# HGRN's levels and the DeltaNet inverse's block products as matmuls of 32 columns, in four strips of the array

## The chip, the core and the metric

The kernel runs on one core of one Trainium2 chip. The metric is the device time of one execution in microseconds; the median of three runs stands for a kernel, and one more execution was profiled. TensorE (PE in the profile; its weight loads are listed apart as PEld) does matmuls into PSUM, VectorE (DVE), ScalarE (ACT) and GpSimd (POOL) work on what it leaves, SyncE (SP) issues the DMAs.

## The reference, cut to what matters

One layer of a decoder trunk: 2048 tokens of width 1024, in f32. After an input projection, four heads go through a gated delta rule (DeltaNet) and four through HGRN2; then come the output projection, an MLP and a gated embedding. The change touches the inside of the two mixers.

```python
# DeltaNet, per chunk of tokens
decay = exp(where(causal, gc[:, None] - gc[None, :], -inf))
lmat  = (k_beta @ k.T) * decay
a_mat = eye + where(strict, lmat, 0)          # unit lower triangular
u, w  = solve(a_mat, v_beta), solve(a_mat, k_beta * exp(gc))
...
# HGRN2, per chunk: a decay for every one of the 128 state channels d
pair = exp(where(causal, b[:, None] - b[None, :], -inf))
att  = einsum('id,jd,ijd->ij', q, k, pair)
o    = att @ v + (q * exp(b)) @ s
...
# what follows
mix = concat(o_a, o_b);  h = x + rms_norm(mix @ w_out)
h  = h + rms_norm(square(relu(rms_norm(h) @ w_up)) @ w_down)
out = h + e * sigmoid(h @ w_gate)
```

## The kernel before

All large products run as matmuls of 128 rows by 128 weight columns by 512 moving columns, with operands split into a high and a low f32r part (`mm`, `mmo`, `u`, `d`, `mmg` in the profile). The small products inside the mixers are plain f32 (`F32` tiles); one of these in the program is two matmuls, each with a weight load, in the trace.

The work goes quarter by quarter (`q`, 512 tokens, four chunks of 128). For each head eight projections of 24 large matmuls are run; after every eighth of these matmuls (`tick`), and half way between (`half`), an agenda lets the generators of the mixers go one step further. So TensorE's order is written by hand: projections of one head with the short products of heads before strewn in, at the places that `A_STEPS` (DeltaNet, `gdn_mixer`) and `B_STEPS` (HGRN, `hgrn_mixer`) name. TensorE and SyncE run in that order; VectorE's, ScalarE's and GpSimd's order in the mixers is set by a scheduler.

*HGRN.* `att` of a chunk of 128 tokens is made in levels, s = 1, 2, 4, ..., 64 (`LEVELS`): at each, pairs of blocks of s tokens, late queries against early keys, both multiplied up to the border between the blocks. The first step of the loop (`lev == 1`) multiplies each chunk's 128 keys with the odd halves of the queries for s = 1 and s = 2 at once (2 x 64 columns, `both`), the others multiply 128 packed `keys` with the 2 x 64 late queries, for two c. Of these products only blocks on the diagonal are wanted; a mask (`mask[lev]`) lets just those through when VectorE copies them to `att` (`copy_predicated`). At s = 4, 8, 16 and 32 a strip of 32 keys meets only 32 of the 128 columns; at s = 64 it is all.

*DeltaNet.* The inverse of the triangular matrix of 128 is made from inverses of its 32-blocks (`xn`, and transposed `xt`), which VectorE solves. Two steps then join blocks to 64 (`um[5]`, `part[5]`: `psp5`, `psx5`, `pst5`) and to 128 (`um[6]`, `part[6]`: `psp6`, `psd6`); each product is run by `pairs` for two pairs of chunks with all 128 weight columns, and ScalarE or VectorE copies out the blocks of 32 or 64 that are wanted.

*PSUM.* Eight banks of [128, 512] f32: `pm` 2 (projections), `po` 2 (outputs), `pp` 4, from which norms, transposes, the DeltaNet products and all HGRN levels (`at_...`) take a bank in turn.

Of the kernel before, what the change touches and what calls it, by code (L numbers as in the profile page):

```python
# [10 lines left out]
F32 = mybir.dt.float32  # L11
# [6 lines left out]
PSUM = bass.MemoryType.PSUM  # L18
DRAM = bass.MemoryType.DRAM

P = 128
# [3 lines left out]
QT = 512  # L25
NQ = T // QT
NC = QT // P
# [4 lines left out]
SB = 32  # L32
NB = P // SB
# [63 lines left out]
def trunk(ctx, tc, x, xT, pT, vecs, w_in, w_ab, gdn_a_log, gdn_dt_bias, w_out, w_up, w_down,  # L97
          w_ple, w_gate, consts, out):
    nc = tc.nc
    V, S, G, PE = nc.vector, nc.scalar, nc.gpsimd, nc.tensor  # L100
# [6 lines left out]
    sm = ctx.enter_context(tc.tile_pool(name="sm", bufs=3))  # L107
    dr = ctx.enter_context(tc.tile_pool(name="dr", bufs=1, space=DRAM))
    pm = ctx.enter_context(tc.tile_pool(name="pm", bufs=2, space=PSUM))
    pp = ctx.enter_context(tc.tile_pool(name="pp", bufs=4, space=PSUM))  # L110
    ph = pp
    po = ctx.enter_context(tc.tile_pool(name="po", bufs=2, space=PSUM))

    def bank(name, pool=None):
        return (pool or pm).tile([P, QT], F32, tag="ps", name=name)

    def blk(c):
        return slice(c * P, (c + 1) * P)

    mixers = ctx.enter_context(ExitStack())  # L120
    cm = mixers.enter_context(tc.tile_pool(name="cm", bufs=1))
    cst = cm.tile([P, N_CONST, P], F32, name="cst")
    rows = cp.tile([N_ROWS, P], F32, name="rows")
# [333 lines left out]
    with mixers as mctx:  # L457
# [12 lines left out]
        um = {lev: mp.tile([P, NC // 2, P], F32, name=f"um{lev}") for lev in (5, 6)}  # L470
        part = {lev: mp.tile([P, NC // 2, P], F32, name=f"part{lev}") for lev in (5, 6)}
# [148 lines left out]
        halves = [slice(0, P // 2), slice(P // 2, P)]  # L620

        def rows_of(g):
            return slice(g * SB, (g + 1) * SB)

        def gdn_mixer(q, h, live):

            n = f"g{q}_{h}"
# [8 lines left out]
            both = sm.tile([P, 2, NC], F32, tag="tail", name=f"tail_{n}")  # L636
# [111 lines left out]
            V.transpose(flat(xt), flat(xn))  # L748
            yield

            def pairs(out, lhsT, rhs):
                for p in range(2):
                    PE.matmul(out[:, p], lhsT[:, p], rhs[:, p], start=True, stop=True)

            def two(t):
                return t.rearrange("p (n two) i -> p n (two i)", two=2)
# [3 lines left out]

            def ends(t):
                return bass.AP(t.tensor, t.offset, [list(t.ap[0]), [P, 2], [3 * SB, 2], [1, SB]])

            def half_bank(name):
                return bank(f"{name}_{n}", pp)[:, : QT // 4].rearrange("p (a i) -> p a i", a=2)

            psp = half_bank("psp5")
            pairs(psp, um[5], ends(xn))  # L770
            for g in range(NB):
                S.activation(part[5][rows_of(g), :, rows_of(g ^ 1)], psp[rows_of(g), :, rows_of(0 if g % 2 else 1)],
                             AF.Copy)
            yield
            psx, pst = half_bank("psx5"), half_bank("pst5")
            pairs(psx, two(xt), ends(part[5]))
# [20 lines left out]
            for c in range(NC):  # L797
                s = state[h]
# [38 lines left out]
        def hgrn_mixer(q, h, live):  # L837
# [26 lines left out]
            for lev, s in enumerate(LEVELS):  # L864
# [4 lines left out]
                if lev == 1:  # L869
                    ps0 = bank(f"at_{n}_d", ph)[:, : QT // 2]  # L870
                    PE.matmul(ps0, one, own, start=True, stop=True)
                    ps1 = bank(f"at_{n}_{lev}", ph).rearrange("p (c n) -> p c n", c=NC)
                    for c in range(NC):
                        PE.matmul(ps1[:, c, :], k[:, blk(c)], both[:, :, c * P // 2 : (c + 1) * P // 2],
                                  start=True, stop=True)
                    chunks = ps1.rearrange("p (a b) n -> p a b n", a=2)
                    eye = bass.AP(ident.tensor, ident.offset, [list(ident.ap[0]), [1, 2], [0, 2], [2, P // 2], [1, 1]])
                    V.tensor_tensor(side_of_chunks(columns_of, 1, False),
                                    ps0.rearrange("p (a b n s) -> p a b n s", a=2, b=2, s=1), eye, ALU.mult)
                    V.tensor_tensor(side_of_chunks(columns_of, 1, True), chunks[:, :, :, : P // 2, None],  # L880
                                    mask[0][:, None, None, :, None].broadcast_to([P, 2, 2, P // 2, 1]), ALU.mult)
                    ps = chunks[:, :, :, P // 2 :]
                else:

                    ps = bank(f"at_{n}_{lev}", ph)[:, : QT // 2].rearrange("p (a b n) -> p a b n", a=2, b=2)
                    for c in range(2):
                        queries = bass.AP(qq.tensor, qq.offset + c * P + s,
                                          [list(qq.ap[0]), [QT // 2 - s, 2], [2 * s, P // (2 * s)], [1, s]])
                        PE.matmul(ps[:, :, c, :], keys[:, blk(c)], queries, start=True, stop=True)  # L889
# [229 lines left out]
        with tc.manual_schedule(engines={mybir.EngineType.SP}):  # L1119
# [826 lines left out]
```

## Time and profile before

| | |
|---|---|
| median of 3 runs | 2665.27 us (2663.72 to 2666.59) |
| profiled execution | 2665.86 us, span of its instructions 2664.1 us |
| PE busy | 2637.0 us (99%), 12745 matmuls |
| PEld (weight loads) busy | 2209.8 us (83%) |
| DVE / ACT / POOL busy | 1968.0 us (74%) / 1468.8 us (55%) / 136.4 us (5%) |
| granted TensorE clock | 1.00 throughout |
| DMA | 573.51 MB, mean 215 GB/s |

The profile is of one execution. Busy time of PE counts overlapping matmuls once, from the start of one to its modelled end, so that 99% says that TensorE is never without work and not that it works at its peak. In rows of groups the columns are: line, engine, operation, output<-inputs, rows*columns of the array and the moving operand, count | busy us, mean ns of one | idle us of the engine before them. In rows of the timeline: start in us from the span's start, us, engine, line, operation, and so on. The mixers run from about 66 to 1107 us; the rest of the output projection, the MLP and the gate follow.

### The profile page before, as it was taken

What the parts mean: (1) busy time and instruction counts of PE and PEld (TensorE: products, weight loads), DVE (VectorE), ACT (ScalarE), POOL (GpSimd) and SP (SyncE); (2) the same over time, 40 slices, a digit from 0 to 9 for tenths busy, and PEclk for the clock granted to TensorE, in tenths of its full rate; (3) what the DMA queues carried; (4) which work ended last, traced back from release to release, by engine and by line L of the source; (5) the groups of instructions that cost most, each with busy time, mean ns of one, the idle gap of its engine ahead of it and who ended that gap; (6) DMA issues with size and microseconds to landing.
All of it is one profiled execution on the core that took longest, in us unless ns stands there. A gap on an engine that the chain in (4) does not pass through costs nothing.

```text
span 2664.1 us, 38284 instructions
## 1 busy us (share of the span) xinstructions
PE 2637.0 (99%) x12745; PEld 2209.8 (83%) x12745; DVE 1968.0 (74%) x4029; ACT 1468.8 (55%) x2991; POOL 136.4 (5%) x147
## 2 busy tenths in 40 slices
PE   8999999999999999999999999999999999999999
PEld 6888888888888888877888888888888888888887
DVE  7778777786677677578988867767877765468775
ACT  6666555465455456566565555555554555565431
POOL 0000000000000000010000000001000001101000
PEclk9999999999999999999999999999999999999999
DMA  8787777667666775682766476666544465677663
GB/s 281 274 261 256 241 268 238 227 225 240 218 212 221 234 220 176 203 250 102 242 213 202 164 242 219 213 204 207 199 171 145 160 236 187 198 253 250 209 224 124
DMA packets 267766, 573.51 MB, mean 215 GB/s; under 512 B 55578, under 2 KB 60152, under 8 KB 250416
## 3 DMA queue, kind: packets, MB, share of 16 engines
q1 hardware_dynamic: 265264, 566.86, 63.9%
q0 software_dynamic: 2304, 4.20, 0.9%
q8 instruction: 101, 1.65, 0.3%
q14 instruction: 97, 0.79, 0.1%
HBM read 410.57 MB, written 160.37 MB: 214 GB/s over the span
## 4 chain that ended last, share of the span: by engine, by line
PE 60%; DMA 3%; DVE 2%; ACT 1%; issue 1%; SPq 0%; POOL 0%; DVEq 0%; ACTq 0%; POOLq 0%
PE d L1171 23%; PE u L1171 23%; PE mmg L1171 7%; PE mm L1139 3%; PE mmo L1022 1%; PE mme L199 1%; DMA mixT<-mixd 1%; DMA yod<-yo 1%; DMA yo<-in_xT_dram 0%; DVE t L173 0%; DVE acc_o L242 0%; DMA sys_g<-ud_g 0%; DMA wd<-in_w_down_dram 0%; PE at_h L889 0%; DMA ud_g<-u_g 0%
## 5 line engine op out<-in xcount | busy, mean ns | idle before, releaser
L1139 PE MATMUL mm<-xt,w 128*128 128x512 f32 x3072 | 783.6, 400 | 1.3 <-DVE w L173 0.8
L1139 PEld LDWEIGHTS mm<-xt,w 128*128 128x128 f32 x3072 | 553.3, 189 | 102.0 <-issue 1.3
L1171 PE MATMUL d<-db,da 128*128 128x512 f32 x2688 | 612.8, 389 | 0.0
L1171 PEld LDWEIGHTS d<-db,da 128*128 128x128 f32 x2688 | 504.5, 188 | 104.8
L1171 PE MATMUL u<-t,wu 128*128 128x512 f32 x2604 | 591.2, 389 | 0.0
L1171 PEld LDWEIGHTS u<-t,wu 128*128 128x128 f32 x2604 | 488.7, 188 | 101.5
L226 DVE TENSOR_TENSOR db<-db 128x512 fp32r<-128x512 f32 x224 | 159.3, 711 | 58.5 <-ACT db L225 57.9
L1569 DVE TENSOR_TENSOR u<-u,u 128x512 f32<-128x512 f32 x224 | 150.1, 681 | 51.3 <-PE u L1171 49.7
L225 ACT ACTIVATE db<-db 128x512 fp32r<-128x512 f32 x224 | 141.0, 629 | 65.6 <-DMA db<-hid 60.4
L1171 PE MATMUL mmg<-h2T,wg 128*128 128x512 f32 (+1 forms) x792 | 174.7, 383 | 0.0
L1171 PEld LDWEIGHTS mmg<-h2T,wg 128*128 128x128 f32 x792 | 145.5, 188 | 29.1
L1612 ACT ACTIVATE u<-u 128x512 f32<-128x512 f32 x128 | 80.8, 631 | 152.3 <-DVE u L1569 151.6
L173 DVE TENSOR_TENSOR da<-da 128x512 fp32r<-128x512 f32 x128 | 95.4, 745 | 88.8 <-ACT da L172 85.5
L172 ACT ACTIVATE da<-da 128x512 fp32r<-128x512 f32 x128 | 80.5, 629 | 126.1 <-DMA da<-sumd 106.5
L1171 PE MATMUL mmo<-mixT,w_out 128*128 128x512 f32 x600 | 138.4, 390 | 1.5 <-DVE w_out L173 1.1
L1171 PEld LDWEIGHTS mmo<-mixT,w_out 128*128 128x128 f32 x600 | 112.2, 188 | 26.6 <-DVE w_out L173 2.3
L172 ACT ACTIVATE wu<-a 128x512 fp32r<-128x512 f32 x124 | 75.1, 624 | 54.6 <-DMA a<-in_w_up_dram 52.7
L173 DVE TENSOR_TENSOR wu<-a,wu 128x512 fp32r<-128x512 f32 x124 | 85.8, 694 | 9.3 <-ACT wu L172 9.1
L173 DVE TENSOR_TENSOR da<-dr,da 128x512 fp32r<-128x512 f32 x96 | 68.2, 710 | 22.9 <-ACT da L172 21.4
L1613 ACT ACTIVATE u<-u 128x512 f32<-128x512 f32 x128 | 80.4, 628 | 3.0
L172 ACT ACTIVATE da<-dr 128x512 fp32r<-128x512 f32 x96 | 60.5, 631 | 30.5 <-DMA dr<-in_w_down_dram 19.6
L242 POOL TENSOR_TENSOR acc_y<-acc_y,sq_y 128x512 f32<-128x512 f32 x28 | 37.9, 1355 | 757.8 <-ACT sq_y L241 757.8
(391 smaller groups left out, 3810.8 us busy)
## 6 DMA issues: line engine op xcount, KB each, us to landing
w<-cache_in SPq DMA_DIRECT2D x96, 1024.0 KB
db<-hid SPq DMA_DIRECT2D x224, 256.0 KB
cache_in<-w SPq DMA_DIRECT2D x32, 1024.0 KB
hid<-u SPq DMA_DIRECT2D x128, 256.0 KB
da<-sumd SPq DMA_DIRECT2D x128, 256.0 KB
a<-in_w_up_dram SPq DMA_DIRECT2D x124, 256.0 KB
hid<-ht SPq DMA_DIRECT2D x96, 256.0 KB
dr<-in_w_down_dram SPq DMA_DIRECT2D x96, 256.0 KB
```

Of the source, the lines that this page charges most:

```text
L172: S.activation(t[:, 0], raw, AF.Copy)
L173: eng.tensor_tensor(t[:, 1], raw, t[:, 0], ALU.subtract)
L199: PE.matmul(ps, a, b, start=i == 0, stop=i == n - 1)
L225: S.activation(t[:, 0], plain(t), AF.Copy)
L226: V.tensor_tensor(t[:, 1], plain(t), t[:, 0], ALU.subtract)
L242: eng.tensor_tensor(acc, acc, sq, ALU.add)
L1022: PE.matmul(ps, w[:, term // 2, k, :], xin[q][k][:, term % 2, :], start=i == 0, stop=i == 3 * KD - 1)
L1139: PE.matmul(ps, *terms[i], start=i == 0, stop=i == nt - 1)
L1171: PE.matmul(ps, a, b, start=start, stop=stop)
L1569: V.tensor_tensor(c[new], c[old], ps, ALU.add)
L1612: S.activation(c[k], c[k], AF.Relu)
L1613: S.activation(c[k], c[k], AF.Square)
```

## The change

The products of the levels up to s = 32, and all block products of the inverse, are no longer matmuls of 128 weight columns. A new helper `strip(g, ...)` runs a matmul of 32 weight columns at column position 32 g of the array, which writes PSUM's partitions 32 g to 32 g + 31; a product is given as four strips, and each strip gets only those moving columns that are read later: 32 of 128 in the levels, 32 of 64 or 64 of 128 in the inverse. Blocks that nobody reads are left out (`psx5`: two strips, not four). The level s = 64 stays as it was.

The levels no longer take a bank from `pp`: they write one bank of their own, `at_all`, set to zero once; the first step uses all of it, those after it its two halves in turn. `pp` has three banks while the mixers run, and four again (a new pool) behind them. What VectorE and ScalarE do with the results is the same.

```diff
-    pp = ctx.enter_context(tc.tile_pool(name="pp", bufs=4, space=PSUM))
-    ph = pp
...
+    pp = mixers.enter_context(tc.tile_pool(name="pp", bufs=3, space=PSUM))
+    ph = pp
+    at_all = mixers.enter_context(tc.tile_pool(name="pa", bufs=1, space=PSUM)).tile([P, QT], F32, name="at_all")
+    V.memset(at_all, 0.0)
...
+        def strip(g, out, lhsT, rhs):
+
+            PE.matmul(out, lhsT, rhs, start=True, stop=True, tile_position=(0, g * SB))
...
-            def pairs(out, lhsT, rhs):
+            def in_halves(out, lhsT, rhs, other):
                 for p in range(2):
-                    PE.matmul(out[:, p], lhsT[:, p], rhs[:, p], start=True, stop=True)
+                    for g in range(NB):
+                        to = halves[g // 2 ^ other]
+                        strip(g, out[rows_of(g), p, to], lhsT[:, p, rows_of(g)], rhs[:, p, to])
...
-            pairs(psp, um[5], ends(xn))
+            for p in range(2):
+                for g in range(NB):
+                    strip(g, psp[rows_of(g), p, rows_of(1 - g % 2)], um[5][:, p, rows_of(g)],
+                          two(xn)[:, p, rows_of(0 if g % 2 else NB - 1)])
...
-            pairs(psx, two(xt), ends(part[5]))
-            pairs(pst, part[5], two(xt)[:, :, SB : 3 * SB])
+            for p in range(2):
+                for g in range(NB):
+                    strip(g, pst[rows_of(g), p, rows_of(g % 2)], part[5][:, p, rows_of(g)],
+                          two(xt)[:, p, rows_of(1 + g % 2)])
+                for g in (1, 2):
+                    strip(g, psx[rows_of(g), p, rows_of(g - 1)], two(xt)[:, p, rows_of(g)],
+                          part[5][:, p, rows_of(0 if g == 1 else NB - 1)])
...
-            pairs(psp, um[6], two(xn))
+            in_halves(psp, um[6], two(xn), 1)
...
-            pairs(psd, part[6], two(xt))
+            in_halves(psd, part[6], two(xt), 0)
...
-                    ps1 = bank(f"at_{n}_{lev}", ph).rearrange("p (c n) -> p c n", c=NC)
+                    near = [slice(j * SB // 2, (j + 1) * SB // 2) for j in range(NB)]
+                    ps1 = at_all.rearrange("p (c n) -> p c n", c=NC)
                     for c in range(NC):
-                        PE.matmul(ps1[:, c, :], k[:, blk(c)], both[:, :, c * P // 2 : (c + 1) * P // 2],
-                                  start=True, stop=True)
+                        for j in range(NB):
+                            strip(j, ps1[rows_of(j), c].rearrange("p (l n) -> p l n", l=2)[:, :, near[j]],
+                                  k[:, c * P + j * SB : c * P + (j + 1) * SB],
+                                  both[:, :, c * P // 2 : (c + 1) * P // 2][:, :, near[j]])
...
-                    ps = bank(f"at_{n}_{lev}", ph)[:, : QT // 2].rearrange("p (a b n) -> p a b n", a=2, b=2)
+                    ps = at_all[:, lev % 2 * QT // 2 : (lev % 2 + 1) * QT // 2].rearrange("p (a b n) -> p a b n", a=2, b=2)
                     for c in range(2):
-                        queries = bass.AP(qq.tensor, qq.offset + c * P + s,
-                                          [list(qq.ap[0]), [QT // 2 - s, 2], [2 * s, P // (2 * s)], [1, s]])
-                        PE.matmul(ps[:, :, c, :], keys[:, blk(c)], queries, start=True, stop=True)
+                        start = qq.offset + c * P + s
+                        if 2 * s == P:
+                            queries = bass.AP(qq.tensor, start, [list(qq.ap[0]), [QT // 2 - s, 2], [1, s]])
+                            PE.matmul(ps[:, :, c, :], keys[:, blk(c)], queries, start=True, stop=True)
+                            continue
+                        for j in range(NB):
+                            out = ps[rows_of(j), :, c, near[j]]
...
+                            strip(j, out, keys[:, c * P + j * SB : c * P + (j + 1) * SB], queries)
...
+    pp = ctx.enter_context(tc.tile_pool(name="pq", bufs=4, space=PSUM))
```

Two places of TensorE's order show it. The first is in the first quarter, where the projections of head 1 carry the second level of head 0's HGRN (`at_h_0_2`), a transpose of head 1's keys (`t_kg`), and then the first block product of head 0's inverse (`psp`) with the third level. Rows give line, output<-inputs, output rows x moving columns, and how many in a row. Before:

```order
L1139 MATMUL mm_0_1_1289<-xt_2_489,w_0_1_1158 128x512 x2
L889 MATMUL at_h_0_2_1298<-qk_h_0_978,keys_h_0_1_1254 128x2x64 x2
L1139 MATMUL mm_0_1_1289<-xt_2_489,w_0_1_1158 128x512
L1139 MATMUL mm_0_1_1289<-xt_3_506,w_0_1_1158 128x512 x3
L1139 MATMUL mm_0_1_1289<-xt_4_522,w_0_1_1158 128x512 x3
L1139 MATMUL mm_0_1_1289<-xt_5_538,w_0_1_1158 128x512
L595 MATMUL t_kg_1_1319<-cst,y_kg_1_1216 128x128 x4
L1139 MATMUL mm_0_1_1289<-xt_5_538,w_0_1_1158 128x512 x2
L1139 MATMUL mm_0_1_1289<-xt_6_554,w_0_1_1158 128x512 x3
L1139 MATMUL mm_0_1_1289<-xt_7_557,w_0_1_1158 128x512 x3
L753 MATMUL psp_g_0_1349<-xn_g_0_1202,um_575 128x64 x2
L889 MATMUL at_h_0_3_1356<-qk_h_0_978,keys_h_0_2_1302 128x2x64 x2
```

The same place in the changed kernel, where the line of all strips is that of the helper, L629:

```order
L1167 MATMUL mm_0_1_1305<-xt_2_494,w_0_1_1163 128x512 x2
L629 MATMUL at_all<-qk_h_0_983,keys_h_0_1_1270 32x2x16 x8
L1167 MATMUL mm_0_1_1305<-xt_2_494,w_0_1_1163 128x512
L1167 MATMUL mm_0_1_1305<-xt_3_511,w_0_1_1163 128x512 x3
L1167 MATMUL mm_0_1_1305<-xt_4_527,w_0_1_1163 128x512 x3
L1167 MATMUL mm_0_1_1305<-xt_5_543,w_0_1_1163 128x512
L597 MATMUL t_kg_1_1340<-cst,y_kg_1_1221 128x128 x4
L1167 MATMUL mm_0_1_1305<-xt_5_543,w_0_1_1163 128x512 x2
L1167 MATMUL mm_0_1_1305<-xt_6_559,w_0_1_1163 128x512 x3
L1167 MATMUL mm_0_1_1305<-xt_7_562,w_0_1_1163 128x512 x3
L629 MATMUL psp_g_0_1370<-xn_g_0_1207,um_580 32x32 x8
L629 MATMUL at_all<-qk_h_0_983,keys_h_0_2_1323 32x2x16 x8
```

Nothing is moved against the projections: where two matmuls of 128 output rows stood, eight of 32 rows stand, and where a product of the inverse and a level follow each other, one stretch of 16. The second place is one head later, on TensorE again, where the inverse's second and third product (`psx`, `pst`) stand before a level. Before:

```order
L753 MATMUL psx_g_1_2050<-part_577,xt_g_1_1873 128x64 x2
L753 MATMUL pst_g_1_2051<-xt_g_1_1873,part_577 128x64 x2
L889 MATMUL at_h_1_3_2062<-qk_h_1_1553,keys_h_1_2_1999 128x2x64 x2
L1139 MATMUL mm_0_2_2084<-xt_0_455,w_0_2_1889 128x512 x3
L1139 MATMUL mm_0_2_2084<-xt_1_472,w_0_2_1889 128x512 x3
```

And in the changed kernel:

```order
L629 MATMUL pst_g_1_2134<-xt_g_1_1934,part_582 32x32 x4
L629 MATMUL psx_g_1_2133<-part_582,xt_g_1_1934 32x32 x2
L629 MATMUL pst_g_1_2134<-xt_g_1_1934,part_582 32x32 x4
L629 MATMUL psx_g_1_2133<-part_582,xt_g_1_1934 32x32 x2
L629 MATMUL at_all<-qk_h_1_1614,keys_h_1_2_2082 32x2x16 x8
L1167 MATMUL mm_0_2_2180<-xt_0_460,w_0_2_1950 128x512 x3
L1167 MATMUL mm_0_2_2180<-xt_1_477,w_0_2_1950 128x512 x3
```

Here `pst` and `psx` change places and alternate, six matmuls become twenty, again in one stretch. Over the whole order there are 82 such stretches: 62 of 16 strip matmuls, 16 of 20 and 4 of 8.

More of the change, by code (lines that the diff above doesn't have):

```diff
@@ L759, in pair_bank @@
                 return bank(f"{name}_{n}", pp)[:, : QT // 2].rearrange("p (a i) -> p a i", a=2)
-            def ends(t):
-                return bass.AP(t.tensor, t.offset, [list(t.ap[0]), [P, 2], [3 * SB, 2], [1, SB]])
             def half_bank(name):
@@ L883, in hgrn_mixer @@
                 else:
-                    ps = bank(f"at_{n}_{lev}", ph)[:, : QT // 2].rearrange("p (a b n) -> p a b n", a=2, b=2)
+                    ps = at_all[:, lev % 2 * QT // 2 : (lev % 2 + 1) * QT // 2].rearrange("p (a b n) -> p a b n", a=2, b=2)
                     for c in range(2):
-                        queries = bass.AP(qq.tensor, qq.offset + c * P + s,
-                                          [list(qq.ap[0]), [QT // 2 - s, 2], [2 * s, P // (2 * s)], [1, s]])
-                        PE.matmul(ps[:, :, c, :], keys[:, blk(c)], queries, start=True, stop=True)
+                        start = qq.offset + c * P + s
[5 more added lines that the diff above has]
+                            out = ps[rows_of(j), :, c, near[j]]
+                            if s < SB:
+                                queries = bass.AP(qq.tensor, start + j * SB, [
+                                    list(qq.ap[0]), [QT // 2 - s, 2], [2 * s, SB // (2 * s)], [1, s]])
+                            else:
+                                out = ps[rows_of(j), j % 2, c, rows_of(j // 2)]
+                                queries = bass.AP(qq.tensor, start + j % 2 * (QT // 2 - s) + j // 2 * 2 * s,
+                                                  [list(qq.ap[0]), [1, s]])
+                            strip(j, out, keys[:, c * P + j * SB : c * P + (j + 1) * SB], queries)
                 late, early = (side(g, nb, 1, x).broadcast_to([P, 2, m, s]) for x in (True, False))
```

## The prediction

> **What bounds the kernel now.** I read the page first (busy shares, slices, chain), then the windows view of the part of the span in which the changed lines run, then TensorE's waits there, then its groups by line and shape, and last the timeline around single groups, because the price of one short matmul stands in no grouped view.
>
> ```profile
> PE 2637.0 (99%) x12745; PEld 2209.8 (83%) x12745; DVE 1968.0 (74%) x4029; ACT 1468.8 (55%) x2991; POOL 136.4 (5%) x147
> PE 60%; DMA 3%; DVE 2%; ACT 1%; issue 1%; SPq 0%; POOL 0%; DVEq 0%; ACTq 0%; POOLq 0%
> ```
>
> The first line is busy time by engine, the second the shares of the chain that ended last. TensorE is busy all the time and leads the chain; VectorE, the next, is at three quarters.
>
> ```profile
> core 0: us, PE busy (x) PEld busy (x) DVE busy (x) ACT busy (x) POOL busy (x), PEclk, DMA share, GB/s
> 66.00:1107.00 1041.00, 1034.68 (x5690) 889.77 (x5689) 761.14 (x2154) 593.34 (x1538) 57.53 (x66) 1.00 0.70 232
> PE kk_g L683 <- ACT y_qg L574: 2.5, 3, 1.8
> PE psc_g L810 <- ACT w_g L807: 1.1, 2, 0.7
> ```
>
> Here is the stretch from 66 to 1107 us, in which the mixers run, and the two longest of TensorE's waits in it (total, times, longest). Of 1041 us TensorE idles 6.3, at a granted clock of 1.00. No other engine sets the pace, so a microsecond added to or taken from TensorE's stream here moves the end by a microsecond. The question is only what the stream costs before and after.
>
> **What is taken out.** The groups of matmuls that the change cuts, and the timeline of TensorE's matmuls around three of them:
>
> ```profile
> L889 PE MATMUL at_h<-qk_h,keys_h 128*128 128x128 f32 x320 | 50.8, 281 | 0.7 <-DVE acc_vg L566 0.7
> L874 PE MATMUL at_h<-hb_h,qk_h 128*128 128x128 f32 x128 | 16.9, 275 | 0.0
> L753 PE MATMUL pst_g<-xt_g,part 128*128 128x64 f32 x64 | 9.8, 275 | 0.0
> L753 PE MATMUL psp_g<-xn_g,um 128*128 128x128 f32 x64 | 9.7, 274 | 0.0
> L753 PE MATMUL psd_g<-xt_g,part 128*128 128x128 f32 x64 | 9.7, 274 | 0.0
> L753 PE MATMUL psp_g<-xn_g,um 128*128 128x64 f32 x64 | 9.0, 262 | 0.4 <-DMA xn_g<-xd_g 0.4
> L753 PE MATMUL psx_g<-part,xt_g 128*128 128x64 f32 x64 | 8.9, 261 | 0.0
> 302.45 0.55 PE L753 MATMUL psx_g<-part,xt_g 128*128 128x64 f32 x4
> 302.84 0.61 PE L753 MATMUL pst_g<-xt_g,part 128*128 128x64 f32 x4
> 303.29 0.66 PE L889 MATMUL at_h<-qk_h,keys_h 128*128 128x128 f32 x4
> 307.43 0.61 PE L753 MATMUL psp_g<-xn_g,um 128*128 128x128 f32 x4
> 307.87 0.61 PE L889 MATMUL at_h<-qk_h,keys_h 128*128 128x128 f32 x4
> 308.32 0.60 PE L595 MATMUL t_kg<-cst,y_kg 128*128 128x128 f32 x4
> ```
>
> A plain f32 matmul of the program is two weight loads and two matmuls in the trace (psx is two in the program, x4 here); I call a load with its matmul a pair. The mean of one (275 ns) is latency and no price, as they are pipelined; the price is the distance of starts. Four pst pairs take 303.29 - 302.84 = 0.45 us, four psp pairs 0.44, four at_h pairs 308.32 - 307.87 = 0.45: 0.111 us a pair, and the same for 64 moving columns (pst) as for 128 (at_h). So with 64 columns it isn't the moving columns that cost, it is the load of 128 columns of weights. Taken out are the 128 pairs of L874, 256 of the 320 of L889 (the sixth level stays as it is) and five groups of 64 of L753: 704 pairs, 704 x 0.111 = 78.1 us.
>
> **What is put in.** Each HGRN head gets 16 strip matmuls for the first level and 8 for each of the next four, 48; each DeltaNet head 8 + 8 + 4 + 8 + 8 = 36. Times 16 heads each: 1344, and as they are plain f32, 2688 pairs with a load of 32 columns and 32 (in 512 of the pairs 64) moving ones. The work is not less in pairs but 3.8 times as many, so all hangs on the price of a narrow pair; break-even without anything else is 78.1 / 2688 = 29 ns. The trace has no narrow pair. The nearest is the small transpose of the decays, which loads 36 rows of 128 columns and moves 36:
>
> ```profile
> 552.17 0.39 PE L280 MATMUL nrm_g<-hl_g,ones 128*128 128x512 f32 x1
> 552.49 0.14 PEld L542 LDWEIGHTS ps_gb<-cst,gb 36*128 36x128 f32 x1 [0.25 <-issue]
> 552.49 0.25 PE L542 MATMUL ps_gb<-cst,gb 36*128 36x36 f32 x1
> 552.55 0.14 PEld L542 LDWEIGHTS ps_gb<-cst,gbb 36*128 36x128 f32 x1
> 552.58 0.23 PE L542 MATMUL ps_gb<-cst,gbb 36*128 36x36 f32 x1
> 552.61 0.14 PEld L542 LDWEIGHTS ps_gb<-cst,gb 36*128 36x128 f32 x1
> 552.67 0.14 PEld L542 LDWEIGHTS ps_gb<-cst,gbb 36*128 36x128 f32 x1
> 552.86 2.11 PE L1139 MATMUL mm<-xt,w 128*128 128x512 f32 x8
> L753 PEld LDWEIGHTS psx_g<-part,xt_g 128*128 128x128 f32 x64 | 9.6, 191 | 1.4
> L595 PEld LDWEIGHTS t_kg<-cst,y_kg 128*128 128x128 f32 x64 | 7.9, 140 | 1.8
> L1171 PE MATMUL d<-db,da 128*128 128x512 f32 x2688 | 612.8, 389 | 0.0
> ```
>
> Its four loads start 0.18 us from first to last, 60 ns a pair. A transpose's load takes 140 ns of latency, an ordinary one 191, 51 more for the same 128 columns; and 111 - 60 is 51 too. So I read: 128 columns loaded once cost about 51, loaded the ordinary way about twice that, and 9 are fixed. For 32 columns: 9 + 102 / 4 = 35 ns, which is an estimate from these rows. From below, everything scales with the columns: 111 / 4 = 28 ns, or less if strips overlap (a rival below). From above, 60 ns may be a floor for any pair, whatever its size. I take 35, since the two load rows agree on the slope. 2688 x 0.035 = 94.1 us. The 512 pairs that move 64 columns I price alike, as moving hid behind loading in the pst row; if it doesn't, they go to some 60 ns, 13 us more.
>
> The Trainium skill, TensorEngine Tiling (Array Packing), section Instruction Overhead, speaks against the change: a matmul has some 60 cycles of overhead, and one should not take the tiling factor from a dimension that is already small. At the 2.4 GHz that the same skill's page TensorE: Matmul & The Clock Gate gives for the array (its table of specifications) this would be an estimate of 25 ns a pair, 67 us and a sum of about 2683; no narrow matmul is in this trace to test it.
>
> **Entering and leaving the strips.** The same rows show a second price. L280's matmul starts at 552.17; a 512-column matmul costs 612.8 / 2688 = 0.228 us (row of d), so the array is free at 552.40. Yet the first load of ps_gb starts at 552.49, though elsewhere loads run under the matmuls (PEld is busy 83% beside PE's 99%), and its row names nothing that it waited for (0.25, "issue"). After ps_gb eight mm end at 552.86 + 2.11 = 554.97; with a latency of 0.39 the last started at 554.58, so at 0.228 each the first really streamed from 554.58 - 1.60 = 552.98 on. Between 552.40 and 552.98 lie 0.58 us for four pairs worth 0.24: 0.33 us are lost going into this shape of the array and out of it. The t_kg transposes above, of 128 rows, lose nothing of the kind (at_h to t_kg 0.45), so it isn't the transposing. I take 0.33 for strips too. In the changed order the strip matmuls stand in 82 unbroken stretches (a level next to a block product counts once): 82 x 0.33 = 27.1 us. Bounds: 0, if strips of columns switch without emptying the array, and 0.5 if the load behind is exposed longer, 41. The Trainium skill, the same page, section Key Properties, says that a change of the tiling mode drains the engine; that column strips are such a change is its statement, no run here shows it yet.
>
> **Banks and the rest.** The rotating pool falls from 4 banks to 3 while the levels no longer use it. Following each bank's last reader through the trace in the new order, only one kind of place comes short, psx/pst behind a norm:
>
> ```profile
> 555.19 0.61 PE L753 MATMUL pst_g<-xt_g,part 128*128 128x64 f32 x4
> 555.47 0.59 ACT L282 ACTIVATE osq_g<-nrm_g 1x512 f32<-1x512 f32 x1
> L896 DVE COPY_PREDICATED att_h<-cst,at_h x96: 414/440/743, 108.9 to 1064.3; 128x256 f32<-128x256 uint32 x96
> ```
>
> There ACT reads the norm's bank until 556.06, and pst would wait for 0.87 us behind it, with the mm queued behind both; it occurs twice, 1.7 us at most, less as the stream gets longer. The levels' own bank is written in halves by turns, so only the second level can meet its reader, the predicated copy of 0.44 us: 16 x 0.44 = 7 us at most, nothing as a rule, since mm lies between two levels. One memset of the bank runs on VectorE before TensorE has data. VectorE and ScalarE keep their instructions in slightly another order; with TensorE's waits at 6 us in all I give it ±5. For these I take +1.
>
> **Sum.** The profiled execution took 2665.9 us (span 2664.1), 0.6 above the median. -78.1 + 94.1 + 27.1 + 1 = +44: 2710 on that execution, 2709 on the median, 1.7% slower.
>
> **Rivals.**
> 1. *A narrow pair costs as much as the smallest pair seen*, 60 ns: load, 0.03, matmul, 0.03, the next load (552.55, 552.58, 552.61), as if load and matmul didn't overlap when both are short. 2688 x 0.060 = 161 us; +111, 2777. For it: the only measured row of the kind. Against: that row is explained by its 128 loaded columns.
> 2. *No fixed part, or no price for the switch.* 28 ns a pair is 75.3 us, +25, 2690; or 35 ns without the 27 us, +17, 2682. For it: large matmuls show little fixed cost. Against: the decays' rows.
> 3. *Strips run side by side, and it gets faster.* If four neighbouring pairs, which stand on four different strips, share one load and one stream, a pair costs 35 / 4 = 9 ns: 24 us, -26, 2639. It decides below (78.1 - 28.1) / 2688 = 18.6 ns a pair. The Trainium skill, TensorEngine Tiling, Key Properties, has different tiles load and multiply in parallel, which would be this. For it: the order does rotate the strips; psx to pst shows that moving hides behind loading. Against: two passes of one strip follow each other before the next strip's, which with in-order matmuls leaves one load per pair on the path.
> 4. *Between 2 and 3*, 17 to 20 ns a pair, within 0.2% (5.3 us, about what a measurement of this kernel tells from no change).
>
> **Chances.** Forecast (30 to 45 ns) 0.34, rival 1 (and up from 45) 0.22, rival 2 0.18, rival 3 0.19, rival 4 0.07. So faster 0.19, same 0.07, slower 0.74. The range goes from 2655, which takes in rival 4 and the mild end of rival 3 (15 ns), to 2782 above rival 1; outside are most of rival 3 and a floor beyond 62 ns.
>
> **What would show it.** Right: the strips' loads 33 to 38 ns apart in the timeline, a load after each stretch that starts late with "issue" as its reason and about 0.33 us lost, TensorE's window of the mixers longer by 44 us and still idle for under 10, everything behind it as long as now. Wrong: starts of strips under 19 ns apart, or all four at once (rival 3); 60 apart (rival 1); the load of a strip ahead under an mm (no switch); or idle time before pst or at_all with ACT or DVE as releaser, over 5 us in all.

## The result, and the profile after

| | before | after |
|---|---|---|
| median, runs beside each other | 2665.93 us (4 runs, 2663.72 to 2666.96) | 2650.68 us (4 runs, 2647.74 to 2652.85) |
| profiled execution, its span | 2665.86 us, 2664.1 us | 2650.4 us, 2648.3 us |
| matmuls on PE | 12745 | 14729 |

The ratio is 0.9943, with a 95% interval of 0.9926 to 0.996. The changed kernel is 15.2 us faster; I had forecast 43 us slower, and 2655 as the lower end. The direction was wrong. Run again on two other chips (`after_again` and `after_third` below) it lay 8.3 and 11.7 us under the kernel before, so the gain is 8 to 15 us.

The page of the changed kernel, busy time by engine and the shares of the chain that ended last:

```profile
PE 2615.3 (99%) x14729; PEld 2159.7 (82%) x14729; DVE 1967.0 (74%) x4030; ACT 1467.4 (55%) x2991; POOL 138.1 (5%) x147
PE 67%; DVE 3%; DMA 3%; issue 2%; ACT 1%; POOL 0%; SPq 0%; DVEq 0%; POOLq 0%; ACTq 0%
```

TensorE still sets the end, with 1984 matmuls more and 22 us less of busy time. The other engines do what they did.

The windows view (length, then PE, PEld, DVE, ACT and POOL busy, granted clock, DMA share, GB/s) for the mixers, which now end 14 us earlier, at 1093 us; and TensorE's longest waits in that stretch (total, times, longest):

```profile
66.00:1093.00 1027.00, 1015.07 (x7692) 840.78 (x7691) 764.43 (x2161) 594.26 (x1541) 58.49 (x66) 1.00 0.72 236
```

```profile
PE kk_g L689 <- ACT y_qg L576: 3.1, 4, 1.2
PE psc_g L823 <- ACT w_g L820: 2.2, 2, 1.2
PE kk_g L688 <- DVE xn_g L792: 2.0, 1, 2.0
...
PE at_all L629 <- DVE att_h L924: 0.6, 1, 0.6
```

TensorE idles 11.9 us in its mixers where it idled 6.3. The row of `at_all` is all that the levels' own bank costs here (0.6 us), and no row names `pst`. What grew are waits for VectorE's and ScalarE's chains in other places of the mixers: the stream got shorter, they did not.

Now the price of a narrow pair. The timeline of the stretch of twenty strip matmuls (40 pairs) in the changed kernel, the second place of the order above, first TensorE's matmuls and then its loads:

```profile
300.08 1.09 PE L1167 MATMUL mm<-xt,w 128*128 128x512 f32 x4
301.10 0.28 PE L629 MATMUL pst_g<-xt_g,part 128*32 128x32 f32 x9
301.19 0.20 PE L629 MATMUL psx_g<-part,xt_g 128*32 128x32 f32 x2
301.20 0.22 PE L629 MATMUL pst_g<-xt_g,part 128*32 128x32 f32 x2
...
301.26 0.22 PE L629 MATMUL at_all<-qk_h,keys_h 128*32 128x32 f32 x1
301.28 0.20 PE L629 MATMUL pst_g<-xt_g,part 128*32 128x32 f32 x2
...
301.38 0.30 PE L629 MATMUL at_all<-qk_h,keys_h 128*32 128x32 f32 x12
301.61 0.96 PE L1167 MATMUL mm<-xt,w 128*128 128x512 f32 x3
```

```profile
300.32 0.41 PEld L1167 LDWEIGHTS mm<-xt,w 128*128 128x128 f32 x2
301.10 0.17 PEld L629 LDWEIGHTS pst_g<-xt_g,part 128*32 128x32 f32 x9 [0.36 <-issue]
```

The last of the four mm ends at 300.08 + 1.09 = 301.17; with 0.40 of latency (the mean of mm, 401 ns, in the groups below) it started at 300.77, and at 0.228 us the array was free at 301.00. Behind the stretch, the last of three mm started at 301.61 + 0.96 - 0.40 = 302.17, so the first streamed from 301.71. Between lie 0.71 us. Less the 0.33 that the prediction gave to entering and leaving, 0.38 us are left for 40 pairs: **9.6 ns a pair**, not 35. The load row shows the predicted late start ("issue"). Nine pst matmuls lie within 0.28 us of each other although each takes about 0.20, and a level's first product (`at_all`, 301.26) starts before the last `pst` (301.28 and later): the strips don't keep the program's order among each other.

The groups of the changed kernel, where the mean of one is latency again and says nothing of the price, but the small busy time does, as overlapping matmuls count once:

```profile
L1167 PE MATMUL mm<-xt,w 128*128 128x512 f32 x3072 | 785.4, 401 | 1.0 <-DVE w L175 0.9
...
L629 PE MATMUL at_all<-hb_h,qk_h 128*32 128x32 f32 x512 | 7.3, 199 | 0.0
```

The 512 pairs of the first level were 128 wide pairs and 16.9 us before; they are 7.3 now.

I did the working of the 0.71 us at all 82 stretches, from the start of the last large matmul ahead to the first streamed one behind. Together they took 129.1 us before and 106.7 after, **22.4 us less**. The other short matmuls of the mixers take 3.1 us more and the large ones there 0.9, nearly all of it waits; the start of the program lies some 2 us later at 50 us and is level again by 75 us. At 1050 us the changed kernel is 16.8 us ahead and at the end 15.8.

### The profile page after: what moved, and what is told of

Same layout as the page of the kernel before. It is cut to its first block, busy times and chain, and to the rows that moved or that the text cites. A ratio compares the mean times of both kernels' runs of the same rounds, so it can differ in the third digit from the quotient of the medians.

```text
span 2648.3 us, 42218 instructions
## 1 busy us (share of the span) xinstructions
PE 2615.3 (99%) x14729; PEld 2159.7 (82%) x14729; DVE 1967.0 (74%) x4030; ACT 1467.4 (55%) x2991; POOL 138.1 (5%) x147
## 4 chain that ended last, share of the span: by engine, by line
PE 67%; DVE 3%; DMA 3%; issue 2%; ACT 1%; POOL 0%; SPq 0%; DVEq 0%; POOLq 0%; ACTq 0%
PE d L1200 23%; PE u L1200 23%; PE mm L1167 9%; PE mmg L1200 7%; PE mmo L1050 1%; PE mme L201 1%; DMA ud_g<-u_g 0%; DMA mixT<-mixd 0%; DMA yo<-in_xT_dram 0%; DMA xs<-in_x_dram 0%; POOL yo L1286 0%; DVE t L175 0%; DVE acc_o L244 0%; PE psc_g L823 0%; PE psa_g L813 0%
```

## Experiments

All are edits of the changed kernel unless said otherwise. "Strips" is the sum over the same stretches in the profiled run, against the kernel before. Ratios are against the kernel before on the same chip.

**1. Are the strips parallel because they stand by turns?** `grouped` puts all products of a strip behind each other (the same in the inverse's products):

```diff
-                    for c in range(NC):
-                        for j in range(NB):
+                    for j in range(NB):
+                        for c in range(NC):
...
```

> The changed kernel with the same strip matmuls in another order: all of strip 0 of a product first, then all of strip 1, and so on, instead of the strips by turns. Theory (side by side: the load and the stream of a pair on one strip run beside those of the next three strips, so that four pairs share the price of one, some 38 ns): pairs of one strip can't overlap, a narrow pair costs 30 to 38 ns in place of 9.6, and 2688 pairs make the kernel 55 to 75 us slower than the changed one, 2705 to 2725. Rival (a narrow pair is cheap by itself, whatever strip stands next to it): no difference, 2651.

2663.83 us (10 runs), ratio 0.9992 (0.9982 to 1.0001); strips -12.3 us. Neither came: its strips save 10 us less than the changed kernel's, and it lies only 3.4 us below the kernel before, but it is far from 35 ns a pair. The first level's stretch in the timeline, of this kernel and then of the changed one:

```profile
105.81 0.90 PE L629 MATMUL at_all<-hb_h,qk_h 128*32 128x32 f32 x32
106.64 0.73 PE L1168 MATMUL mm<-xt,w 128*128 128x512 f32 x2
```

```profile
107.50 0.46 PE L629 MATMUL at_all<-hb_h,qk_h 128*32 128x32 f32 x32
107.89 3.94 PE L1167 MATMUL mm<-xt,w 128*128 128x512 f32 x16
```

0.83 us against 0.39 for the same 32 pairs, eight in a row on each strip. In the stretch of psx, pst and a level, with four to eight in a row, it costs less (14 ns a pair against 9.6). So the order matters, and strips still overlap across a few pairs of another. Whether it is the distance that one strip can run ahead which decides was not measured by itself.

**2. Do the moving columns count?** `allcols` lets the levels' strips move all 128 columns:

```diff
-                            strip(j, ps1[rows_of(j), c].rearrange("p (l n) -> p l n", l=2)[:, :, near[j]],
+                            strip(j, ps1[rows_of(j), c, :],
                                   k[:, c * P + j * SB : c * P + (j + 1) * SB],
-                                  both[:, :, c * P // 2 : (c + 1) * P // 2][:, :, near[j]])
+                                  both[:, :, c * P // 2 : (c + 1) * P // 2])
...
+                            queries = bass.AP(qq.tensor, start,
+                                              [list(qq.ap[0]), [QT // 2 - s, 2], [2 * s, P // (2 * s)], [1, s]])
+                            strip(j, ps[rows_of(j), :, c, :], keys[:, c * P + j * SB : c * P + (j + 1) * SB], queries)
```

> The changed kernel, in which the levels' strips stream all 128 moving columns, as before the change, and not the 32 that are read. Theory (side by side): four strips stream at the same time, so four pairs cost the 0.107 us of one stream, 27 ns a pair in place of 9.6; 1536 pairs of the levels make +27 us, 2678. Rival (cheap by itself, one after the other): a pair costs its own stream of 0.107 us, 1536 x 0.097 = +150 us, 2800. A third reading (fixed price per pair, no matter how many columns): 2651.

2681.61 us (4 runs), ratio 1.0064 (1.0049 to 1.0079), as side by side expected; strips +11.1 us. The same stretch:

```profile
107.46 1.08 PE L629 MATMUL at_all<-hb_h,qk_h 128*32 128x128 f32 x32
108.47 3.70 PE L1161 MATMUL mm<-xt,w 128*128 128x512 f32 x15
```

1.01 us instead of 0.39: 19 ns more a pair, about 27 in all. The loads are the same 32 columns, so here the moving columns set the price and not the load, and the cut of the columns is a part of the change that it can't do without: with strips over all columns it would be a loss.

**3. One strip alone.** `one_strip` leaves out strips 1 to 3 of the levels:

```diff
-                        for j in range(NB):
+                        for j in range(1):
...
```

> The changed kernel, in which the levels leave out strips 1 to 3 (three quarters of their products are missing in the result). Theory (each strip is a queue of its own, a pair takes some 32 ns on one strip, and four strips run at once): the 384 pairs left on one strip take as long as the 1536 on four, within 3 us of the changed kernel, 2648 to 2652; in the first level's stretch the pairs stand some 32 ns apart. Rival (a pair costs 9.6 ns whatever strip it is on): 1152 x 0.0096 = 11 us less, 2640, and the pairs of one strip 10 ns apart.

2657.83 us (4 runs), ratio 0.9963 (0.9949 to 0.9978); the changed kernel on the same chip (`after_again`, below) had 0.9963 too. A level that stands alone between large matmuls, here and in the changed kernel:

```profile
105.70 3.94 PE L1167 MATMUL mm<-xt,w 128*128 128x512 f32 x16
109.57 0.31 PE L629 MATMUL at_all<-qk_h,keys_h 128*32 128x32 f32 x4
109.81 2.11 PE L1167 MATMUL mm<-xt,w 128*128 128x512 f32 x8
```

```profile
108.69 3.14 PE L1167 MATMUL mm<-xt,w 128*128 128x512 f32 x13
111.76 0.33 PE L629 MATMUL at_all<-qk_h,keys_h 128*32 128x32 f32 x16
112.03 1.19 PE L1167 MATMUL mm<-xt,w 128*128 128x512 f32 x4
```

By the working above, the gap between the large matmuls is 0.455 us for 4 pairs on one strip and 0.476 for 16 on four. Less 0.33, that is 31 ns a pair on one strip and 9 on four. The single starts, which these rows merge, say it without a subtraction. In `one_strip` the four pairs start 53, 31 and 32 ns after each other. In the changed kernel four pairs start within 20 ns, 6 to 7 ns apart, and each such four again follows the one before by 53, 31 and 32 ns. Three quarters of a level's work cost 0.02 us to add. This is the mechanism: each strip takes a pair in about 31 ns, and the four do so at the same time. The Trainium skill, TensorEngine Tiling (Array Packing), section Key Properties, says that tiles work independently and load and multiply in parallel; the runs bear that out. Its section Instruction Overhead, by which I had worked out an estimate of 25 ns a pair, holds at most for one strip: four strips get through a pair in 9.6 ns on average.

**4. The halves of the change.** `levels_only` runs the inverse's products as before, `inverse_only` the levels and the banks:

```diff
-            in_halves(psp, um[6], two(xn), 1)
+            pairs(psp, um[6], two(xn))
...
```

> The change for HGRN's levels alone (with their own bank); the inverse's products are matmuls of 128 columns as before. 384 wide pairs go (42.6 us), 1536 narrow ones come (14.8 at 9.6 ns), and there are 80 stretches of strips at 0.33 us for going in and out (26.4). Theory (the switch has its price per stretch): about nothing is left, -1 us, 2664 to 2666 with the rest. Rival (no switch price, or one that is hidden): -28 us, 2638.

2667.33 us (10 runs), ratio 1.0002 (0.9992 to 1.0011); strips -4.8 us.

> The change for the inverse's products alone; the levels are matmuls of 128 columns in the pool of four banks, as before. 320 wide pairs go (35.5 us), 1152 narrow ones come (12 us, those of 64 columns at 12.6 ns), 64 stretches (21 us). Theory (a price per stretch): -2 to -3 us, 2663. Rival (no switch price): -23 us, 2643. With levels_only it tells whether the two halves add up: by the theory they don't, both together save more, as they share stretches.

2669.99 us (10 runs), ratio 1.0017 (1.0007 to 1.0026); strips -0.9 us. Apart the halves are worth nothing, together 8 to 15 us (the whole was not run on the chip of the halves). There are 80 stretches in the one and 64 in the other, but 82 in the whole, since a level stands next to a block product nearly everywhere: 62 entries into the strips and exits are shared, 62 x 0.33 = 20.5 us. And -4.8 - 0.9 - 20.5 = -26.2, near the -22.4 of the whole.

**5. The switch by itself.** Two kernels get 64 spare wide products, one in each product group of the inverse: `spare_first` ahead of its strips, `spare_mid` between the halves of it, which makes 146 stretches. The edit of `spare_mid`:

```diff
             for p in range(2):
+                spare(p)
                 for g in range(NB):
...
+            def spare(p):
+                if p == 1:
+                    PE.matmul(spares[-1], um[6][:, 0], um[6][:, 1], start=True, stop=True)
```

(p == 0 in `spare_first`.)

> The changed kernel with one spare plain f32 product of 128 by 128 columns (two pairs, 0.22 us) directly before each of the inverse's four strip groups, written to an unused part of their bank: 64 products, outside the stretches. All theories: 64 x 0.22 = +14 us on the changed kernel, 1.000 to 1.001 of before. It is the control of the next.

2670.02 us (10 runs), ratio 1.001 (1.0001 to 1.0019), as expected.

> The same 64 spare products, but in the middle of the strip groups, so that there are 146 stretches of strips in place of 82. Theory (0.33 us for going in and out of the strips, each time): 64 x 0.33 = 21 us more than the control, +35 on the changed kernel, 1.008 to 1.009 of before. Rival (no such price; what stands before and behind a stretch is the wait for operands): the same as the control.

2681.76 us (4 runs), ratio 1.0055 (1.0041 to 1.0069): 11.7 us over `spare_first`, where I expected 21. The same place in `spare_first` and in `spare_mid`:

```profile
310.72 0.85 PE L1180 MATMUL mm<-xt,w 128*128 128x512 f32 x3
311.41 0.39 PE L776 MATMUL psp_g<-um 128*128 128x128 f32 x2
311.73 0.43 PE L629 MATMUL psp_g<-xn_g,um 128*32 128x64 f32 x16
311.97 0.31 PE L629 MATMUL at_all<-qk_h,keys_h 128*32 128x32 f32 x16
312.21 0.66 PE L597 MATMUL t_kg<-cst,y_kg 128*128 128x128 f32 x4
```

```profile
306.04 3.92 PE L1180 MATMUL mm<-xt,w 128*128 128x512 f32 x16
309.90 0.32 PE L629 MATMUL psp_g<-xn_g,um 128*32 128x64 f32 x8
310.14 0.49 PE L776 MATMUL psp_g<-um 128*128 128x128 f32 x2
310.56 0.32 PE L629 MATMUL psp_g<-xn_g,um 128*32 128x64 f32 x8
310.70 0.31 PE L629 MATMUL at_all<-qk_h,keys_h 128*32 128x32 f32 x16
310.94 0.66 PE L597 MATMUL t_kg<-cst,y_kg 128*128 128x128 f32 x4
```

From the end of the last mm (310.72 + 0.85 - 0.40 + 0.228 = 311.40, and 309.79) to the first t_kg it is 0.81 and 1.15 us: 0.34 for one more exit and entry. In 60 of the 64 places it is 0.29 to 0.37, with a median of 0.33, which would make 21 us over all; in the other four, other waits differ, one by 3 us, and the sum is some 16 us. The price of the switch stands: going into strips and out of them costs what the transpose of the decays costs. That the time grew by 11.7 only goes with waits elsewhere: in the profiled runs the other short matmuls waited 6.8 us less in the longer stream. TensorE's losses in the mixers are partly absorbed, as its gains are partly given back.

**6. The banks.** `own_bank` is the kernel before with the banks of the changed one:

```diff
-    pp = ctx.enter_context(tc.tile_pool(name="pp", bufs=4, space=PSUM))
...
+    pp = mixers.enter_context(tc.tile_pool(name="pp", bufs=3, space=PSUM))
...
-                    ps1 = bank(f"at_{n}_{lev}", ph).rearrange("p (c n) -> p c n", c=NC)
+                    ps1 = at_all.rearrange("p (c n) -> p c n", c=NC)
```

> The kernel before with the banks of the changed one (the levels' own bank, three in the pool) and all products 128 columns wide as before. Theory (the lost microseconds of the change, 22 gained in the strips and 15 measured, are in part bank waits): +2 to +3 us, 1.001. Rival (banks cost nothing): 1.000, no waits on psx's or the levels' readers in the profile.

2671.68 us (11 runs), ratio 1.0019 (1.001 to 1.0028): some 5 us, against my +1. Its profiled run, the fastest of the eleven, has no row that shows the price, only waits for the bank's reader of 0.5 us:

```profile
PE at_all L895 <- DVE att_h L902: 0.5, 2, 0.3
```

By the starts of the same large matmuls that run is 1.5 us ahead of the kernel before at the end of the mixers and loses 2.2 us in the 200 us behind them. So the 5 us were not found in the mixers; where they lie stays open.

> The changed kernel with psx and pst in one bank (each uses a quarter of one), so that a DeltaNet head takes one bank less from the pool of three. Theory (the bank kernel's +5 us are waits for a bank): 2 to 4 us below the changed kernel, 0.993 to 0.995 of before. Rival (the pool doesn't matter once the levels have left it): the changed kernel's 0.995 to 0.996.

`shared` puts psx and pst in one bank (`psx, pst = pxt[:, 0], pxt[:, 1]`), so that three banks of the pool go further. 2654.01 us (5 runs), ratio 0.9952 (0.9939 to 0.9966), against `after_again`, the changed kernel once more:

> The changed kernel once more, to have it on the same chip as the next kernels. All theories: 0.994 of the kernel before, as measured.

2658.19 us (6 runs, two at 2650.8 and four at 2657.9 to 2659.6), ratio 0.9963 (0.995 to 0.9975). The two can't be told apart.

**7. The last wide product of the levels.** `diag` is `shared` with the product for the diagonal (L884) in four strips too, with 64 of its 256 moving columns each:

```diff
-                    PE.matmul(ps0, one, own, start=True, stop=True)
+                    for j in range(NB):
+                        strip(j, ps0[rows_of(j)].rearrange("p (c n) -> p c n", c=NC)[:, :, near[j]], one[:, rows_of(j)],
+                              own.rearrange("p (c n) -> p c n", c=NC)[:, :, near[j]])
...
```

For it, the attention of all heads stands in one tile that is set to zero once, the diagonal's operand gets a tile of its own, and a scratch tile of ScalarE has one buffer in place of two. What these cost was not measured apart.

> The changed kernel with two more steps. The diagonal product (all-ones weights times 256 columns, two matmuls of 213 ns per head) becomes four strips of 64 columns, of which only the own block is copied, standing directly before the first level's strips; and psx and pst share one bank. Theory (in a stretch that is there anyway a strip costs no switch): 0.43 us of wide matmul per head become 8 pairs at 12 ns, 16 x 0.33 = 5.3 us off; the bank some 2 us of waits; 6 us below the changed kernel, 0.992 of before. Rival (four small copies on VectorE in place of one hold up the second level, or the queue is the limit): no gain, 0.994.

2654.12 us (5 runs), ratio 0.9957 (0.9945 to 0.9969). The first level's stretch, worked out as above, fell from 1.245 to 0.971 us, 4 us over all sixteen heads, and no time came of it. TensorE's longest wait in its mixers:

```profile
PE at_all L630 <- DVE att_all L930: 5.1, 4, 1.4
```

The four small copies of the diagonal stand on VectorE ahead of the copy that frees the levels' bank. So `diag2` has them behind it, where they overwrite entries of the second level (its result lacks these), and `diag3` as predicated copies that leave those entries alone:

> The diagonal in strips and the shared bank, as in the first try, with the four small copies of the diagonal behind the first level's predicated copy on VectorE and not ahead of it. Theory (in the first try the strips won 4 us and the second level, which waits for that copy in the own bank, gave them back): the waits of at_all on att_all fall from 5.1 us to 1 or less, 0.993 of before, 3 to 5 us below the changed kernel. Rival (the microseconds are lost somewhere in the mixers whatever TensorE saves, as VectorE's and ScalarE's chains are next): 0.995 to 0.996.

2651.82 us (5 runs), ratio 0.9947 (0.9934 to 0.9959); the wait above fell to 1.1 us, so the place of the small copies made most of it.

> The changed kernel with psx and pst in one bank and the product for the diagonal in four strips, copied to the attention behind the level's predicated copy, cell by cell through a mask, so that the second level's entries stay. Theory (the first-level stretch falls from 1.245 to 0.97 us, 4 us in all, and the late copies keep TensorE from waiting for them): 0.993 of the kernel before, 2 to 4 us under the changed kernel. Rival (the saving goes into waits for VectorE, which has 48 more instructions): no better than the changed kernel, 0.995 to 0.996.

2654.64 us (5 runs), ratio 0.9956 (0.9944 to 0.9968); strips -27.5 us, 5 more than the changed kernel, and waits elsewhere took it back. No version that beats the changed kernel by more than the runs scatter was found.

**8. Who takes it back?** Both kernels without the 96 predicated copies of the levels, 42 us of VectorE:

```diff
-                V.copy_predicated(side_of_chunks(columns_of, s, True),
-                                  mask[lev].rearrange("p (a n s) -> p a n s", a=2, s=s).bitcast(U32)[:, :, None]
-                                  .broadcast_to([P, 2, 2, P // (2 * s), s]),
-                                  ps.rearrange("p a b (n s) -> p a b n s", s=s))
```

> The kernel before, without the 96 predicated copies of the HGRN levels on VectorE (0.44 us each, 42 us of VectorE in the mixers); its attention lacks the levels from s = 2 on. Every matmul stays. Theory (part of the time that the strips save is given back as waits for VectorE's and ScalarE's chains): TensorE waits for little here, 6.3 us in the mixers, so the time falls by 2 to 5 us, to about 2662. Rival (the rest of the saving is lost elsewhere, VectorE has no part in it): within 2 us of the kernel before.

2669.82 us (11 runs), ratio 1.001 (1.0001 to 1.0019): not faster. Its profiled run is level with the kernel before at the end of the mixers (0.2 us later) and loses 3.7 us behind them.

> The changed kernel without the same 96 copies. Theory: with 42 us less on VectorE the strips' saving of 22 us comes through in full, so that this lies 19 to 24 us below the same cut of the kernel before, about 2641, and TensorE's waits in the mixers fall to 6 us or less. Rival: it lies 8 to 15 us below it, as the changed kernel does below the kernel before, about 2651.

2652.88 us (5 runs), ratio 0.9941 (0.9929 to 0.9954). The two differ by 16.9 us; the changed kernel once more on this chip, `after_third`, lay 11.7 us below the kernel before:

> The changed kernel once more, as the measure for the other three: 0.994 to 0.996 of the kernel before, in single runs near 2651 or 2658.

2655.68 us (6 runs, 2647.17 to 2661.33), ratio 0.9953 (0.9939 to 0.9967). 16.9 lies between the two expectations. The strips of `lean_after` give 23.8 us against `lean_before`, and other short matmuls take back 5.8, with ScalarE in the longest row of waits now:

```profile
PE mm L1163 <- ACT part L799: 3.5, 2, 2.1
PE psc_g L823 <- ACT w_g L820: 1.7, 3, 1.0
```

So VectorE's load alone isn't the cause; the longest rows of waits differ from kernel to kernel.

The profiled run of `after_third` (span 2656.3 us) lies 8 us above the first one of the changed kernel, and shows where. It loses 4 us on it in the mixers, and 4.25 us at one place behind them, where the weights of the output projection (`w_out`) are split. TensorE's and ScalarE's rows of its timeline there, and its windows of 4 us:

```profile
1118.17 10.72 PE L1200 MATMUL mmo<-mixT,w_out 128*128 128x512 f32 x46 [0.32 <-DVE w_out L175]
1132.86 7.42 PE L1200 MATMUL mmo<-mixT,w_out 128*128 128x512 f32 x19 [3.97 <-ACT w_out L174]
...
1129.12 0.63 ACT L227 ACTIVATE mixT<-mixT 128x512 fp32r<-128x512 f32 x1 [6.10 <-DMA mixT<-mixd]
1131.75 1.06 ACT L174 ACTIVATE w_out<-raw_out 128x1024 fp32r<-128x1024 f32 x1 [0.51 <-DMA raw_out<-in_w_out_dram]
```

```profile
1132.00:1136.00 4.00, 3.10 (x7) 2.00 (x8) 1.79 (x2) 1.06 (x2) 0.00 (x0) 0.50 1.09 308
1136.00:1140.00 4.00, 4.00 (x14) 3.20 (x13) 2.55 (x5) 3.91 (x8) 0.00 (x0) 0.70 1.05 408
```

ScalarE waits 6.1 us for a tile of the mixers' output that comes back from memory, and only then splits `w_out`; TensorE stands for 4.0 us. Behind it, the granted clock is 0.50 and 0.70. In the first profile the same place reads:

```profile
PE mmo L1200 <- ACT w_out L174: 1.5, 1, 1.5
1124.00:1128.00 4.00, 2.01 (x9) 1.02 (x7) 2.38 (x3) 1.06 (x1) 0.00 (x0) 1.00 1.10 262
```

The wait (first row) was 1.5 us and the clock stayed at 1.00. That the DMA engines are full there (share 1.05 to 1.10) speaks for the transfers as the cause, and as both runs are of the same kernel, the difference isn't the change's doing; no run altered that place, so its cause is only argued. Between 1107 and 1300 us, behind the mixers, the profiled runs of this document lose between 0.5 and 8 us on the profile of the kernel before, `lean_before` with the same code there 3.7. So a few microseconds between two whole times can't be put down to the mixers.

## Why the prediction was wrong

- *What bounds the kernel*: right that TensorE's stream sets the end before and after. That a microsecond taken from it moves the end by a microsecond was too strong: 22.4 us less in the stretches became 15.2, and some 16 us more in `spare_mid` became 11.7.
- *What is taken out*, 0.111 us for each of 704 wide pairs: right. The stretch of psx, pst and a level (12 pairs) takes 1.577 us before, from one large matmul's start to the next, which is 0.228 + 12 x 0.111 = 1.56.
- *What is put in*, 35 ns for each of 2688 narrow pairs: **the step that failed.** 35 was near for a pair on one strip (31 measured), but the two load rows don't explain that number: with the same loads of 32 columns a strip's pair takes 56 ns at 64 moving columns and 109 at 128, so how near it came was in part luck. And I put it on the path four times over: "with in-order matmuls" one load per pair was to stay there. Each strip instead works through its own pairs while the others do the same, and 31 / 4 is 8; measured were 8 to 9.6 ns at 32 moving columns. Rival 3 had this, with 9 ns and 24 us; I gave it 0.19. The term is 94.1 against about 26 us (2688 x 0.0096): 68 us.
- *Moving 64 columns costs as much as 32*: wrong, but small. A psd product alone (16 pairs) has a stretch of 0.792 us; less 0.228 and 0.33 that is 14.6 ns a pair, and its single starts show each strip's pairs 56 ns apart. For 512 pairs it is some 3 us more than at 8 to 9.6.
- *The switch*, 0.33 us in each of 82 stretches, from the transpose of the decays: right in size (0.33 at the median place of `spare_mid` over `spare_first`). The halves apart show what it decides: 144 entries instead of 82 undo the whole gain.
- *Banks*, +1 us: the wait that I had named, of `at_all` for its reader, is there with 0.6 us, the one of `pst` isn't. The banks alone cost 5 us with the old products, of which the waits name 0.5.
- *±5 for the other engines' order*: about right as a size, with a sign that I had not seen. By rival 3's sum -26 were due, the stretches gave -22.4, and the time fell by 15.2. What is missing between the last two is idle time of TensorE at other places: 5.6 us more in the mixers, and 1 us behind them in the profiled run. Why these chains come later was not settled.
- *The lower end*, 2655: the later medians of 2658.19 and 2655.68 lie above it. That says nothing for the mechanism, as this end stood for 15 ns a pair, and 8 to 9.6 were measured.

## What to carry to other kernels

When a small product wastes most of the array's columns, count its price per strip and not per instruction: column strips, set down by turns, work through their pairs at the same time. Here 3.8 times the pairs took a third of the time, the switches aside, and only because each strip moves no more than the columns that are needed. Put strip work next to strip work: each entry and exit cost 0.33 us here, as much as three wide pairs. And don't count on the whole of what a shorter stream saves: here, with two more engines at 55 and 74%, 22.4 us in the stretches became 15.8 of the span in one profile, and 5.6 of the rest were new waits in the mixers.

## What the runs showed of the hardware that was not expected

A matmul of 32 weight columns on its strip is paid by its moving columns: from one start on a strip to the next it is 31 ns at 32 (`one_strip`), 56 at 64 (psd in the changed kernel) and 109 at 128 (`allcols`), the last about as much as a wide pair on the whole array. For the wide pairs 64 and 128 moving columns cost the same 0.111 us. And matmuls of later products start before earlier products on other strips have started (301.26 before 301.28 in the rows above), so with strips TensorE's matmuls here did not start in the program's order.
